# The first layer of a two-layer decoder trunk: operators on VectorE, state products on column parts by turns, a finer and new order of steps

## The chip, the cores and the metric

One Trainium2 chip (trn2), of which the kernel uses one core. The metric is device time in microseconds (us) of one execution, the median of several. The kernel is one launch; weights and activations are float32 in device memory.

## The reference

The reference computes two layers on one sequence of 256 tokens of width 1024, with 256 memory tokens. Each layer is a mixing part and a gated feed-forward block with a causal convolution over three tokens; every part starts from an RMS norm.

- Layer 0 mixes by a diagonal state-space layer (S5) on 768 of the 1024 columns: 48 groups of 16 channels with 64 complex states each. `y_t = Re(C s_t) + d u_t`, `s_t = A s_(t-1) + B u_t`, then `y = gelu(y)` and `y * sigmoid(y @ w_glu)`.
- Layer 1 mixes by causal attention of 12 heads on keys and values of its own.
- In both layers the other 256 columns are four heads of attention to the memory tokens: `softmax(q k^T / 8) v`, with keys and values `rms_norm(mem) @ w_mem_kv`.
- The two parts are joined, multiplied by `w_out` and added to the residual `x`; then `x + (silu(g) * v) @ w_down` with `g, v` from the convolution of `rms_norm(x) @ w_up`.

## The kernel before, in words

Activations lie with the 1024 features on partitions (8 tiles of 128) and the 256 tokens on the free axis. A float32 weight tile is split into an upper half `whi` (ScalarE, L115) and the rest `wlo` (VectorE, L119, or L121 where a gain is multiplied in), and a product is three matmuls (L249 to L251). Weights whose key stands in `NATIVE` are not split: one matmul in native float32, which the trace shows as two records. `Stream` (L82 to L136) loads weight tiles in a fixed list `order` (L199 to L205), two ahead, and splits them four ahead.

Layer 0 (`layer0`, from L590) works in these steps; the letters in brackets are those of the list `ORDER` (L43 to L48).

- Coefficients (L679 to L745) on VectorE: the decay, phase and input factors of the 24 pairs of groups. Powers of the phase factor (`E0`, `E1`; L778 to L801) for 8 and for 16 pairs, in four rounds, the fourth the largest; before, E0 is on VectorE, E1 on GpSimd.
- For each of three sets b of 8 pairs: the input operators (`Xr`, `Xi`; L747 to L758), two products and two sums each; the same transposed on TensorE (`T`, `t`; L766 to L776); the output operators (`V`; L803 to L819), two products and one sum of 128x1024, all nine on GpSimd before.
- The local operator (`l`, L821 to L843): per pair two products of 64 columns and one with the diagonal, into a 32-column part of the array; `L` copies it into place.
- The projection `x @ w_in` (`P`, native; L863 to L873), the mixer input (`u`), its placement (`U`, 16 copies per set, L880 to L889), the states (`S`): matmuls L896 and L897, rotation, two scans, rotation back and sums into `Hs` (L891 to L928).
- The outputs (`Y`): products of `U` with the local operator (L941) and of `Hs` with the output operator (L944) into two column halves, one half after the other; copies, transposes, gelu (`G`).
- Memory keys and values of layer 0 (`K`, native) and of layer 1 (`K1`, split; `m` splits the memory tokens for it), the queries (`q`) and the four memory heads (`A`: `attend`, L493 to L500): scores, softmax (L432 to L452), transposes, and the product with the values (L470, L471), each head alone in its column half.

Inside `tc.manual_schedule` TensorE, VectorE and GpSimd issue their instructions in just this list's order; ScalarE and everything outside it are placed by the scheduler, by priority. The gate with `w_glu`, the output projection and the residual follow outside the list. Layer 1 (L1085 on) has its own list `ORDER1`, placed by priority throughout.

Of the kernel before, what the change touches and what calls it, by code (L numbers as in the profile page):

```python
# [19 lines left out]
T = 256  # L20
# [11 lines left out]
NATIVE = (("mkv", 0), ("win", 0))  # L32
# [23 lines left out]
T_ACT = ((0, 0), (0, 1), (1, 0), (1, 1), (2, 0), (2, 1))  # L56
U_ACT = ((1, 1, 1, 0), (0, 1, 1, 1), (1, 0, 1, 1))
# [4 lines left out]
I I r1 X I I I r2 X I I I r3 Q0 qm Q1 h0 Q2 Q1 h2 K h0 K K X X h3 h2 K h1 R0 h1 h2 K K v v Q0 R1 R0 h3 R1 h0 h4 h5  # L62
h1 h3 v R2 v h7 e0 h10 Q2 h4 h6 h5 h8 h9 h7 h4 v v v h11 R2 v h2 h10 h6 h9 h13 h4 h5 h1 h14 h8 h6 h10 h0 h8 h12 h6
h7 h12 h3 O h11 h7 h13 h9 h14 h11 e1 h8 h12 h15 h15 h9 h13 h10 h12 h14 h13 h15 h5 h11 O O h15 h14 O O z1 O O O z0 z2
z3
"""
ST_DVE = [('k', 1)]
# [72 lines left out]
def _body(ctx, tc, a):  # L140
# [58 lines left out]
    order = [(("win", 0, ks, h), blocks(a["w_in"][0], ks, 512 * h, 512), (len(ks), 512)) for ks, h in W0]  # L199
    order += [(("mkv", l, c), mkv_ap(l, c), (2, 512)) for l in range(2) for c in range(4)]  # L200
    order += [(("glu", ks, b), blocks(a["w_glu"], ks, 256 * b, 256), (3, 256)) for ks, b in GLU]
    order += wout(0) + ffn_order(0) + win(1)
    order += [(("wk", ks, b), blocks(a["w_kv"], ks, 256 * b, 256), (4, 256)) for ks, b in WK]
    order += [(("wv", ks, c), blocks(a["w_kv"], ks, SELF + 384 * c, 384), (2, 384)) for c in range(2) for ks in PAIRS]
    order += wout(1) + ffn_order(1)  # L205
# [161 lines left out]
    def mem_kv(l, bk, mh, ml, ks, new, vm):  # L367
        pk, pv = bk(), bk()
        for k in range(KT):
            if k % 2 == 0:  # L370
                w = W.get(("mkv", l, k // 2))
            o = 512 * (k % 2)
            g = [m if m is None else m[k // 2][:, k % 2] for m in (mh, ml)]
            pairs = [(i, j) for i, j in ((0, 0), (0, 1), (1, 0)) if w[i] is not None and g[j] is not None]
            for m in range(2):
                for i, j in pairs:
                    PE.matmul(pk[:, 256 * m:256 * m + 256], w[i][:, o + 128 * m:o + 128 * m + 128], g[j],  # L377
                              start=k + m + i + j == 0, stop=k == KT - 1, skip_group_check=True)
            for t in range(2):
                for i, j in pairs:  # L380
                    PE.matmul(pv[:, 256 * t:256 * t + 256], g[j][:, 128 * t:128 * t + 128],  # L381
                              w[i][:, o + 256:o + 512], start=k + t + i + j == 0, stop=k == KT - 1,
                              skip_group_check=True)
            yield
# [47 lines left out]
    def softmax(sl, p, causal):  # L432
# [10 lines left out]
        for t in range(2):  # L443
            K = 128 * (t + 1) if causal else 256
            S.activation(P[:, t, :K], p[:, 256 * t:256 * t + K], AF.Exp, bias=nm[:, t:t + 1], scale=HD ** -0.5,
                         accum_out=su[:, t:t + 1])
        r = sm.tile([128, 2], F32, name="r")
# [4 lines left out]
        return P  # L452
# [20 lines left out]
    def head(h, sl, bs, bt, bo, q, k, v, causal, outp, hi, lo):  # L473
# [9 lines left out]
        if i not in outp:  # L483
            outp[i] = [bo("psO"), 0]
# [8 lines left out]
    def attend(heads):  # L493

        n = len(heads)
        for s in range(n + 3):
            for d in range(4):
                if 0 <= s - d < n:
                    next(heads[s - d])
# [771 lines left out]
```

## Time and profile before

| | us |
|---|---|
| median of 3 runs | 694.61 (694.43 to 701.04) |
| the profiled execution | 695.04 |
| its span, first to last instruction | 693.3 |
| TensorE busy | 654.1 (94%) |
| VectorE busy | 565.4 (82%) |
| ScalarE busy | 413.2 (60%) |
| GpSimd busy | 132.9 (19%) |

The profiled execution is one run of the same program with the hardware profiler on. Matmul records overlap (they are pipelined), so their cost is read from start to start, not from their durations. The granted clock of TensorE is given as a share of 2.4 GHz: 0.50 is 1.2 GHz, and a stretch with a value between has some of both.

### The profile page before, as it was taken

Reading aid. Unit: us, or ns where it says so; the run is one execution under the profiler, and the core shown is the slowest. Engines: PE = TensorE matmul, PEld = TensorE weight load, DVE = VectorE, ACT = ScalarE, POOL = GpSimd, SP = SyncE. Lnnn points to the kernel's source line nnn. Section 1 sums busy time; section 2 is a strip of 40 time slices with the busy share of each in tenths; the row PEclk is TensorE's granted clock in tenths of the full one; section 3 lists DMA queues with packets and bytes.
Section 4 is the critical chain, followed back from the end, with each engine's and each line's share of the span. In section 5 each row is a group of like instructions: output and inputs, shape, how many; then the busy total and the mean of one; then the engine's idle time right before and its main releaser. Section 6 shows DMA issues by size and latency. Waiting matters only on the chain.

```text
span 693.3 us, 12668 instructions
## 1 busy us (share of the span) xinstructions
PE 654.1 (94%) x4904; PEld 616.5 (89%) x4904; DVE 565.4 (82%) x1012; ACT 413.2 (60%) x747; POOL 132.9 (19%) x134
## 2 busy tenths in 40 slices
PE   6369899999999999999999998989999999999995
PEld 5358888998899999999999997868999999999984
DVE  7996999796879998888888798974749999888872
ACT  6368625576556665555557579864636666555631
POOL 5795623402300000000001255500300000000000
PEclk9775879999999999999999999899999999999998
DMA  8610133274455555555555544323625555565401
GB/s 315 245 62 1 61 99 99 93 217 148 152 181 184 183 183 181 186 185 182 182 186 156 168 128 140 107 89 122 213 92 182 181 186 183 183 188 187 172 1 61
DMA packets 43259, 105.13 MB, mean 152 GB/s; under 512 B 3776, under 2 KB 14144, under 8 KB 43200
## 3 DMA queue, kind: packets, MB, share of 16 engines
q1 hardware_dynamic: 42624, 103.74, 45.9%
q8 instruction: 38, 0.62, 0.4%
q10 hardware_dynamic: 576, 0.59, 0.2%
q14 instruction: 21, 0.17, 0.1%
HBM read 103.28 MB, written 1.05 MB: 150 GB/s over the span
## 4 chain that ended last, share of the span: by engine, by line
PE 82%; DVE 12%; DMA 2%; issue 2%; ACT 1%; POOL 0%; SPq 0%; DVEq 0%; ACTq 0%
PE psU L250 12%; PE psU L251 12%; PE psU L249 12%; PE acc L557 9%; PE acc L249 7%; PE acc L250 7%; PE acc L251 7%; PE ps L377 2%; DVE wlo L119 2%; PE ps L381 2%; PE ps L838 1%; DMA s5c<-s5b 1%; PE psO L470 1%; DVE X L638 1%; PE psT L458 1%
## 5 line engine op out<-in xcount | busy, mean ns | idle before, releaser
L115 ACT ACTIVATE whi<-wraw 128x1024 fp32r<-128x1024 f32 (+1 forms) x176 | 182.9, 1042 | 142.4 <-PE psU L250 84.9
L119 DVE TENSOR_TENSOR wlo<-wraw,whi 128x1024 fp32r<-128x1024 f32 (+1 forms) x176 | 217.9, 1240 | 26.7 <-PE acc L251 13.1
L250 PE MATMUL psU<-xlo,whi 128*128 128x256 f32 x704 | 198.6, 282 | 1.4 <-DVE xlo L331 1.4
L251 PE MATMUL psU<-xhi,wlo 128*128 128x256 f32 x704 | 197.8, 282 | 0.0
L249 PE MATMUL psU<-xhi,whi 128*128 128x256 f32 x704 | 197.6, 282 | 0.0
L250 PEld LDWEIGHTS psU<-xlo,whi 128*128 128x128 f32 x704 | 132.9, 189 | 2.5 <-DVE xlo L331 1.8
L249 PEld LDWEIGHTS psU<-xhi,whi 128*128 128x128 f32 x704 | 132.7, 189 | 0.7
L251 PEld LDWEIGHTS psU<-xhi,wlo 128*128 128x128 f32 x704 | 132.6, 189 | 0.0
L528 DVE SCALAR_TENSOR_TENSOR y<-u,held,y 128x254 f32<-128x254 f32 (+1 forms) x176 | 77.8, 477 | 1.5 <-ACT y L526 1.5
L521 DVE TENSOR_TENSOR u<-psU,rb 128x512 f32<-128x512 f32 x44 | 30.3, 688 | 32.4 <-PE psU L251 31.3
L526 ACT ACTIVATE y<-u,held 128x256 f32<-128x256 f32 x88 | 47.6, 589 | 13.0 <-DVE u L521 12.9
L269 POOL TENSOR_TENSOR sq<-sq 128x512 f32<-128x512 f32 x5 | 8.0, 1598 | 226.9 <-DVE held L364 179.1
L251 PE MATMUL acc<-ah,wlo 128*128 128x256 f32 x176 | 49.7, 283 | 0.0
L250 PE MATMUL acc<-al,whi 128*128 128x256 f32 x176 | 49.7, 283 | 0.0
L249 PE MATMUL acc<-ah,whi 128*128 128x256 f32 x176 | 49.6, 282 | 0.0
L869 PE MATMUL acc<-xg,wraw 128*128 128x256 f32 x128 | 34.1, 429 | 5.5 <-ACT xg L859 5.5
L869 PEld LDWEIGHTS acc<-xg,wraw 128*128 128x128 f32 x128 | 27.7, 221 | 10.0 <-ACT xg L859 5.5
L288 POOL TENSOR_TENSOR y<-mf,held 128x1 f32<-128x1 f32 x2 | 1.1, 550 | 180.5 <-DVE mf L1215 180.5
L249 PEld LDWEIGHTS acc<-ah,whi 128*128 128x128 f32 x176 | 33.6, 191 | 0.0
L251 PEld LDWEIGHTS acc<-ah,wlo 128*128 128x128 f32 x176 | 33.5, 191 | 0.0
L250 PEld LDWEIGHTS acc<-al,whi 128*128 128x128 f32 x176 | 33.5, 191 | 0.0
L250 PE MATMUL acc<-xlo,whi 128*128 128x256 f32 x112 | 31.7, 284 | 0.0
(271 smaller groups left out, 1475.1 us busy)
## 6 DMA issues: line engine op xcount, KB each, us to landing
wraw<-w_up SPq DMA_DIRECT2D x88, 512.0 KB, 3.4
wraw<-w_down SPq DMA_DIRECT2D x44, 512.0 KB, 3.4
wraw<-w_out SPq DMA_DIRECT2D x16, 512.0 KB, 3.6
wraw<-w_in SPq DMA_DIRECT2D x15, 512.0 KB, 3.5
wraw<-w_mem_kv SPq DMA_DIRECT2D x8, 512.0 KB, 4.2
wraw<-w_kv SPq DMA_DIRECT2D x6, 512.0 KB, 3.7
wraw<-w_kv SPq DMA_DIRECT2D x8, 384.0 KB, 3.4
wraw<-w_glu SPq DMA_DIRECT2D x6, 384.0 KB, 3.5
```

The lines of the kernel that those rows point to most:

```text
L115: self.nc.scalar.activation(hi[:, c], t[:, c], AF.Copy, scale=1.0 if g_ is None else g_)
L119: self.nc.vector.tensor_sub(lo[:, c], t[:, c], hi[:, c].bitcast(F32))
L249: PE.matmul(out, whi, ahi, start=first, stop=False, skip_group_check=True)
L250: PE.matmul(out, whi, alo, start=False, stop=False, skip_group_check=True)
L251: PE.matmul(out, wlo, ahi, start=False, stop=last, skip_group_check=True)
L377: PE.matmul(pk[:, 256 * m:256 * m + 256], w[i][:, o + 128 * m:o + 128 * m + 128], g[j], start=k + m + i + j == 0, stop=k == KT - 1, skip_g ...
L381: PE.matmul(pv[:, 256 * t:256 * t + 256], g[j][:, 128 * t:128 * t + 128], w[i][:, o + 256:o + 512], start=k + t + i + j == 0, stop=k == KT ...
L521: V.tensor_mul(u, v2(p), rb2(rb))
L526: S.activation(y[:, j], u[:, j], AF.Identity, bias=cp(3), scale=cp(2))
L528: V.scalar_tensor_tensor(y[:, j, d:], u[:, j, :T - d], cp(2 - d), y[:, j, d:], op0=ALU.mult, op1=ALU.add)
L557: PE.matmul(dacc[2 * t + h], a_, w_[:, 512 * i:512 * i + 512], start=False, stop=last and a_ is al, skip_group_check=True)
L869: PE.matmul(acc[2 * h + b][:, 256 * (m % 2):256 * (m % 2) + 256], w[:, 512 * i + 128 * m:512 * i + 128 * m + 128], xg[k // 2][:, k % 2], s ...
```

## The change

- Engines: the output operators' products go to VectorE, but for the sum of set 2; the first three rounds of E1 stay on GpSimd and its fourth goes to VectorE, the fourth of E0 goes to GpSimd; of the input operators the real half of set 2 is now GpSimd's instead of the imaginary half of set 0. All of the sums into `Hs` are on VectorE. Copies move between ScalarE and VectorE: eight of the twelve place copies that VectorE had go to ScalarE, one operator half (two copies), one `yc` copy and two `yT` copies go to VectorE.
- States, outputs and local operator are issued by turns on column parts of the array: states as two products of 64 columns each, outputs with the two halves alternating, the local operator over four 32-column parts. The diagonal comes ready from the host, as a 128-row table, instead of being multiplied out on VectorE.
- The second layer's memory projection becomes native: no split of its weights, no split of the memory tokens.
- Order: a new list, with finer steps (projection by halves, powers, output operators, local operator, outputs, softmax in two pieces). The gate, output projection and residual are in the list too. What stands behind the mark `|` is placed by priority. Weight loads are listed by the steps; their order comes out the same.
- Heads: two heads of a pair issue their value products together, alternating between the column halves, in both layers. Layer 1's list is as before but for the doubled softmax step, the pair steps `p` and the steps `x` for its first split.

```diff
-NATIVE = (("mkv", 0), ("win", 0))
+NATIVE = (("mkv", 0), ("mkv", 1), ("win", 0))
 ORDER = """
-P rm0 E0 P rx1 E1 P rx2 E0 P rx3 Xi0 Xr0 E0 V1 u0 t0 V0 V0 Xi1 u1 P B0 T0 D0 V0 Xr1 V1 U1 U0 P U0 l0 U0 T1 E1 U0 E1
-E1 Xi2 Xr2 E0 U1 S0 V1 P t2 S0 T2 S0 L0 U1 L0 P B1 L0 V2 t1 S0 D1 u2 U1 V2 U2 U2 U2 m S1 U2 S2 K S1 K K D2 K rm1 V2
-S1 B2 q l1 S1 L1 L1 rm2 L0 S2 Y0 S2 m S2 K K K K rm3 Y0 K L1 L1 G0 m K1 Y1 G0 Y2 Y1 K1 K1 m Y2 K1 G1 G2 K1 K1 G1 K1
-A G2 A A A A K1 A K1 A
+P E0 P P E1 P P P rm0 E0 Xr0 rx1 P P P rx2 E0 rx3 E0 E1 P Xi0 u0 D0 P U0 T0 U0 P U0 t0 P E1 D2 Xr1 P U0 V0 B0 Xi1 S0
+u1 V0 V0 l0 T1 Xi2 U1 S0 P U1 S0 l0 V2 V1 P V1 L0 V2 t1 K Xr2 B1 S0 L0 T2 U1 K u2 V1 rm1 U2 K U2 U1 L0 L0 Y0 B2 K U2
+t2 U2 E1 S1 V2 l1 D1 l1 l1 l1 L1 rm2 L1 S1 rm3 S2 Y0 S1 S1 K L1 K S2 K S2 Y0 L1 S2 K K1 Y1 K G0 G0 | q Y2 Y2 h1 Y1 h2
+Y1 h1 h3 h3 K1 K1 h0 Y2 h2 G1 h1 G2 h0 K1 K1 h0 K1 G1 h2 G2 h3 h1 h2 h0 K1 h3 K1 g g g g g p1 g0 g0 g g1 p0 g1 p1 K1
+g2 p0 o o o o g2 o o o o z3 z2 z1 z0
 """
-X_POOL = ((0, 1),)
-E_POOL = (1,)
-M_POOL = (1, 2, 3)
-H_DVE = (1,)
-V_DVE = ()
-Y_ACT = (0, 1, 2)
-EVAC_ACT = (0, 1, 2)
-T_ACT = ((0, 0), (0, 1), (1, 0), (1, 1), (2, 0), (2, 1))
-U_ACT = ((1, 1, 1, 0), (0, 1, 1, 1), (1, 0, 1, 1))
+V_POOL = ((2, 2),)
+X_POOL = ((2, 0),)
+E_POOL = ((0, 3), (1, 0), (1, 1), (1, 2))
+H_DVE = (0, 1, 2)
+Y_ACT = (1,)
+EVAC_ACT = (0, 2)
+T_ACT = ((0, 0), (0, 1), (1, 1), (2, 0), (2, 1))
+U_ACT = ((1, 1, 1, 0), (1, 1, 1, 1), (1, 1, 1, 1))
...
-    def pv(out, off, v, PT, causal):
-        c = 128 if causal else 0
-        PE.matmul(out[off:off + 64, :256], v[0], PT[:, 0], start=True, stop=False, skip_group_check=True)
-        PE.matmul(out[off:off + 64, c:256], v[1], PT[:, 1, c:], start=False, stop=True, skip_group_check=True)
+    def pv(out, pair, causal):
+        for t in range(2):
+            c = 128 if t and causal else 0
+            for h in range(2):
+                v, PT = pair[h]
+                PE.matmul(out[64 * h:64 * h + 64, c:256], v[t], PT[:, t, c:], start=t == 0, stop=t == 1,
+                          skip_group_check=True)
...
             for f in range(nf):
+                o = [p[32 * s:32 * s + 32, 128 * f:128 * f + 128] for s in range(4)]
+                for g in range(2):
+                    for s in range(4):
+                        PE.matmul(o[s].rearrange("p (i c) -> p i c", c=32)[:, :, 16 * g:16 * g + 16],
+                                  Bz[i][:, 4 * f + s, g], Vd[i][:, 4 * f + s, g, 0:4], start=g == 0, stop=False,
+                                  tile_position=(0, 32 * s), skip_group_check=True)
                 for s in range(4):
...
+                    PE.matmul(o[s][:, :32], ident[:, 32 * s:32 * s + 32], dsk[:, PC[i][0] // 4 + f], start=False,
+                              stop=True, tile_position=(0, 32 * s), skip_group_check=True)
+                yield
...
             for j in range(8):
-                PE.matmul(pr[:, 64 * j:64 * j + 64], RT[b][0][:, j], U[b][:, j], start=True, stop=True)
-                PE.matmul(pi[:, 64 * j:64 * j + 64], RT[b][1][:, j], U[b][:, j], start=True, stop=True)
+                for ri, p in enumerate((pr, pi)):
+                    for c in HALF:
+                        PE.matmul(p[c, 64 * j:64 * j + 64], RT[b][ri][:, j, c], U[b][:, j], start=True, stop=True,
+                                  tile_position=(0, c.start), skip_group_check=True)
...
-            for f in range(2):
-                for s in range(4):
-                    j = 4 * f + s
...
+            for s in range(4):
+                o = [py[64 * f:64 * f + 64].rearrange("p (i s c) -> p s i c", s=4, c=32)[:, s] for f in range(2)]
+                for f in range(2):
+                    PE.matmul(o[f], U[b][:, 4 * f + s], Tm[pc][:, off + 4 * f + s], start=s == 0, stop=False,
+                              tile_position=(0, 64 * f), skip_group_check=True)
+                for g in range(2):
+                    for f in range(2):
+                        PE.matmul(o[f][:, :, 16 * g:16 * g + 16], Hs[b][:, 4 * f + s, g],
+                                  Vd[pc][:, off + 4 * f + s, g, 1:5], start=False, stop=True,
+                                  tile_position=(0, 64 * f), skip_group_check=True)
...
+        by_hand, by_priority = ORDER.split("|")
+        with tc.manual_schedule(engines=MANUAL):
+            steps(by_hand)
+        steps(by_priority)
```

## Rows read from the trace of the kernel before

**Rows 1.** The page, section 4: the chain that ended last, by engine.

```profile
PE 82%; DVE 12%; DMA 2%; issue 2%; ACT 1%; POOL 0%; SPq 0%; DVEq 0%; ACTq 0%
```

**Rows 2.** Busy time by stretch: PE, PEld, DVE, ACT, POOL, granted clock, DMA.

```profile
60.00:80.00 20.00, 20.00 (x105) 18.38 (x104) 15.06 (x19) 11.82 (x28) 13.64 (x11) 0.73 0.16 46
80.00:100.00 20.00, 18.16 (x89) 16.41 (x88) 19.10 (x22) 9.47 (x22) 11.13 (x10) 0.74 0.22 74
```

**Rows 3.** Timeline of VectorE: start, us, engine, line, operation, count.

```profile
23.72 0.42 DVE L728 TENSOR_TENSOR s5c<-ct 128x72 f32<-128x72 f32 x2
...
28.98 3.00 DVE L638 TENSOR_TENSOR xt<-s5c 128x512 f32<-128x512 f32 x2
32.01 4.62 DVE L638 TENSOR_TENSOR X<-xt 64x512 f32<-64x512 f32 x2
...
46.25 1.31 DVE L638 TENSOR_TENSOR xt<-s5c 128x512 f32<-128x512 f32 x2
47.59 1.40 DVE L638 TENSOR_TENSOR X<-xt 64x512 f32<-64x512 f32 x2
...
58.34 0.19 DVE L638 TENSOR_TENSOR ee<-E 128x16 f32<-128x16 f32 x1
...
59.89 1.05 DVE L638 TENSOR_TENSOR E<-et 128x168 f32<-128x168 f32 x4
...
108.31 0.68 DVE L903 TENSOR_TENSOR rot<-ps,E 128x512 f32<-128x512 f32 x1
...
116.54 2.33 DVE L925 TENSOR_TENSOR H<-rot 64x504 f32<-64x504 f32 x2
```

**Rows 4.** Timeline of TensorE, the first feed-forward matmuls.

```profile
183.07 0.28 PE L249 MATMUL psU<-xhi,whi 128*128 128x256 f32 x1
183.19 0.28 PE L250 MATMUL psU<-xlo,whi 128*128 128x256 f32 x1
```

**Rows 5.** Timeline of GpSimd, two output-operator products.

```profile
29.10 4.66 POOL L635 TENSOR_TENSOR Vd<-s5c 128x1024 f32<-128x1024 f32 x2
```

**Rows 6.** The page, section 5: lower halves of weights on VectorE.

```profile
L119 DVE TENSOR_TENSOR wlo<-wraw,whi 128x1024 fp32r<-128x1024 f32 (+1 forms) x176 | 217.9, 1240 | 26.7 <-PE acc L251 13.1
```

**Rows 7.** Timeline of TensorE, states of set 1 and local operator of 16 pairs.

```profile
79.08 0.39 PE L897 MATMUL ps<-U,RT 128*128 128x64 f32 x2
79.30 0.39 PE L896 MATMUL ps<-U,RT 128*128 128x64 f32 x2
...
100.58 0.41 PE L838 MATMUL ps<-Vd,Bz 128*32 128x64 f32 x4
...
101.10 0.41 PE L838 MATMUL ps<-Vd,Bz 128*32 128x64 f32 x4
```

**Rows 8.** Timeline of TensorE, outputs of set 0 at the change of column half.

```profile
109.47 0.39 PE L944 MATMUL psY<-Vd,H 128*64 128x64 f32 x4
109.70 0.39 PE L941 MATMUL psY<-Tm,U 128*64 128x128 f32 x2
...
109.92 0.32 PE L941 MATMUL psY<-Tm,U 128*64 128x128 f32 x1
...
110.09 0.50 PE L944 MATMUL psY<-Vd,H 128*64 128x64 f32 x5
110.42 0.38 PE L941 MATMUL psY<-Tm,U 128*64 128x128 f32 x2
```

**Rows 9.** Timeline of TensorE, value products of two memory heads of layer 1.

```profile
448.83 0.66 PE L470 MATMUL psO<-PT,held 128*64 128x256 f32 x4
449.31 0.61 PE L471 MATMUL psO<-PT,held 128*64 128x256 f32 x4
```

**Rows 10.** Timeline of TensorE, native memory projection, two k steps.

```profile
115.43 1.03 PE L377 MATMUL ps<-memT,wraw 128*128 128x256 f32 x4
...
117.16 1.03 PE L377 MATMUL ps<-memT,wraw 128*128 128x256 f32 x4
```

**Rows 11.** Timeline of TensorE's weight loads for rows 9.

```profile
448.82 0.20 PEld L470 LDWEIGHTS psO<-PT,held 128*64 128x64 f32 x4 [0.25 <-issue]
```

More of the change, by code (lines that the diff above doesn't have):

```diff
@@ L198, in _body, with by_steps @@
     W0 = [((0,), 0), ((1,), 0)] + [(ks, h) for h in range(2) for ks in PAIRS][1:]
[L199 to L205, printed above, removed]
+    def by_steps(steps, **lists):
+        its = {n: iter(l) for n, l in lists.items()}
+        return [w for s_ in steps.split() if s_ in its for w in next(its[s_], ())]
+    one = lambda l: [[w] for w in l]
+    w0 = [(("win", 0, ks, h), blocks(a["w_in"][0], ks, 512 * h, 512), (len(ks), 512)) for ks, h in W0]
+    mkv = lambda l: [[(("mkv", l, k // 2), mkv_ap(l, k // 2), (2, 512))] if k % 2 == 0 else [] for k in range(KT)]
+    glu = [(("glu", ks, b), blocks(a["w_glu"], ks, 256 * b, 256), (3, 256)) for ks, b in GLU]
+    order = by_steps(ORDER, P=[w0[:2], []] + [p for w in w0[2:] for p in ([w], [])], K=mkv(0), K1=mkv(1), g=one(glu),
+                     o=one(wout(0)))
+    order += ffn_order(0)
+    order += by_steps(
+        ORDER1, I=one(win(1)),
+        K=one([(("wk", ks, b), blocks(a["w_kv"], ks, 256 * b, 256), (4, 256)) for ks, b in WK]),
+        v=one([(("wv", ks, c), blocks(a["w_kv"], ks, SELF + 384 * c, 384), (2, 384)) for c in range(2) for ks in PAIRS]),
+        O=one(wout(1)))
+    order += ffn_order(1)
     W = Stream(nc, order, rawp, hlp, lambda key: [gains[:, 2 + key[1], 2 * key[2] + i:2 * key[2] + i + 1]
@@ L370, in mem_kv @@
             if k % 2 == 0:
[L371 to L374, printed above, removed]
+                w, _ = W.get(("mkv", l, k // 2))
+            o, mk = 512 * (k % 2), mem[k // 2][:, k % 2]
             for m in range(2):
[L376 to L378 removed]
+                PE.matmul(pk[:, 256 * m:256 * m + 256], w[:, o + 128 * m:o + 128 * m + 128], mk, start=k + m == 0,
+                          stop=k == KT - 1, skip_group_check=True)
             for t in range(2):
[L380 to L383, printed above, removed]
+                PE.matmul(pv[:, 256 * t:256 * t + 256], mk[:, 128 * t:128 * t + 128], w[:, o + 256:o + 512],
+                          start=k + t == 0, stop=k == KT - 1, skip_group_check=True)
             yield
@@ L1000, in layer0 @@
             gens[f"Y{b}"] = outputs(b)
[L1001 removed]
+            gens[f"V{b}"] = output_operator(b, sc[1])
             gens[f"U{b}"] = by_place(b)
@@ L1050, in layer0, with steps @@
                 calls[f"{n}{b}"] = lambda f=f, b=b: f(b)
+        gens["g"], gens["o"] = gate(), output0()
+        for b in range(3):
+            gens[f"g{b}"] = gated(b)
+        for b in range(4):
+            calls[f"z{b}"] = lambda b=b: residual0(b)
         for i in range(2):
-            calls[f"l{i}"] = lambda i=i: local_operator(i)
+            gens[f"l{i}"] = local_operator(i)
             gens[f"L{i}"] = put_local_operator(i)
-        with tc.manual_schedule(engines=MANUAL):
-            for s in ORDER.split():
+        def steps(text):
+            for s in text.split():
                 if s in gens:
```

187 lines of the change are left out of this document (79 added, 108 removed).

## The prediction

> **What bounds the kernel now.** I read the chain of waits first. It puts 82% of the span on TensorE and 12% on VectorE [rows 1]; the two feed-forward blocks are matmuls end to end, the diff leaves them alone, and I count nothing there. So I cut the first 200 us into stretches: in 60 to 100 us TensorE looks busy nearly all the time, but its granted clock is only 0.73 and 0.74, that is, a mix of the levels 1.2 and 2.4 GHz, while VectorE is busy for 34 of the 40 us and GpSimd for 25 [rows 2]. The engine timelines then give the two halves of the first layer, and I use two marks to part them. Mark A is the end of the last state product of set 2 on VectorE, 116.54 + 2.33 = 118.9 us [rows 3]. Mark B is the first feed-forward matmul, 183.07 us [rows 4]. Up to A the order is set by VectorE, which starts behind the coefficients at 24.1 us [rows 3]; from A to B TensorE has no gap in its timeline: 64.2 us of matmuls.
>
> **VectorE up to A, step by step.** First its prices, taken where GpSimd is quiet. Half an input operator (Xr or Xi) is two products and two sums: 1.31 + 1.40 = 2.7 us; the same beside GpSimd's long products took 3.00 + 4.62 = 7.6 us [rows 3]. So a long GpSimd instruction costs VectorE more than the work it takes over: two output-operator products on GpSimd took 4.66 us [rows 5], and a 128x1024 product on VectorE takes 1.24 us [rows 6]. The fourth round of powers for 8 pairs took from 58.34 to 60.94, 2.6 us; for 16 pairs I take 4.5, bounds 2.6 (all fixed cost) and 5.2 (all size). One set of states took 108.31 to 116.54 = 8.2 us up to its last sums, and those are now four sums on VectorE, each as long as the 128x512 product at 108.31, 0.68 us: 2.7, together 10.9 us a set [rows 3].
>
> The list in the new order, from 24.1 us to the new A:
> - second and third round of E0: 3.6 (ten instructions of about 0.18 us each, the small ones in [rows 3]);
> - five halves of the input operators, as many as before but other ones: 5 x 2.7 = 13.5;
> - eight output-operator products and sums moved from GpSimd: 8 x 1.2 = 9.6;
> - fourth round of E1: 4.5;
> - three sets of states: 3 x 10.9 = 32.7;
> - three mixer inputs, two operator copies and one output copy of 128x512 at about 0.65: 3.9; one place copy of four instructions instead of twelve: 1.5;
> - two roots with GpSimd's power between them: 4.0 (an estimate; the power alone holds VectorE for about 1 us).
>
> That is 73.3 us. GpSimd keeps one fourth round, one half input operator and one output sum, about 11 us by the prices in [rows 5] and by size, and by the two prices of an input operator VectorE loses about half of that: 6. New A: 24.1 + 73.3 + 6 = 103.4 us, 15.5 earlier. In exchange go the lower halves of the second layer's memory weights (eight instructions), the memory split and the diagonal products; they stand in front of A today and are not in the list. Bounds: 97 with no loss to GpSimd; 137 if the operators run at the disturbed prices (five halves at 7.6, eight products at 2.4: 34 us more).
>
> The order of the weight loads stays as it is, and in 60 to 100 us the DMA engines are busy for 0.16 and 0.22 of the time [rows 2], so a stretch that gets shorter by a sixth finds its weights; the larger diagonal table is one more load of some 100 KB ahead of tables that are needed late.
>
> What ScalarE takes on (eight place copies, fewer evacuations) is hidden as long as it stays under VectorE's list; without that cover the place copies of set 0 would delay the first states by some 2 us.
>
> **TensorE.** Its products get shorter where column parts run side by side.
> - States: two records take 0.22 us, so 32 records cost 3.6 us a set at 2.4 GHz [rows 7]. After the change there are 64 records of half the width.
> - Local operator: a pair, six records, takes 0.52 us at 2.4 GHz [rows 7]; 24 pairs cost 12.3.
> - Outputs: six records take from 109.47 to 109.92, 0.45 us [rows 8], so 48 cost 3.6 us a set.
>
> What does running by turns give? The trace shows it once per set, where the outputs pass from one column half to the other: the first U product of the second half starts at 109.92, just when the last four records of the first half are due, and ten records are through by 110.42 [rows 8]. The last four ran alone, 0.22 us, so the six before them took 0.28 instead of 0.45. The other witness is longer: two heads whose value products the scheduler happened to put next to each other took at most 1.09 us for eight records [rows 9], where eight records in a row take 1.73 (the native projection, rows 115.43 to 117.16 [rows 10]). So the factor lies between 0.5 and 0.63 where it was seen; the other end is 1, no gain. I take 0.55 for two parts and 0.3 for four (estimates; the four-part bound is 0.25 to 1): states and outputs 3 x 1.6 each, local operator 8.6 less. That is 18.2 us of matmuls at 2.4 GHz, 16.6 of them ahead of A (all but the outputs of set 2). Only what stands behind A is counted directly; the rest keeps TensorE off VectorE's path.
>
> Against it, the second layer's memory projection becomes native: a k step costs 1.73 us [rows 10] instead of twelve products at 0.118 (start to start [rows 4]) = 1.42, so 8 x 0.31 = +2.5.
>
> **From A to B.** If nothing else moves ahead of A, what is left is: outputs of set 2 2.0, transposes 0.9, seven k steps 12.1, scores 1.9, head transposes 1.8, two head pairs 2.0 (four single heads cost 4 today), gate 108 x 0.118 = 12.7, output projection 192 x 0.118 = 22.6: 56.0 us. B would be 159.4. The other bound: TensorE has some 64 us of matmuls ahead of A in 98 us, so the seven k steps and the heads could fill its gaps; with all 17.8 us of them gone and 3 us of waiting for the last gate input, 41.2, B would be 144.6. VectorE's own list behind A (gelu, weight splits, heads, gates) comes to about 37 us, so it does not bind first. Since TensorE pays part of its gaps at 1.2 GHz, I take the nearer end: 4 us move ahead. B = 103.4 + 52 = 155.4, 27.7 us earlier; bounds 24 and 38.
>
> **Second layer.** Pairing head products looks like sixteen halved heads, but it mostly exists: both memory pairs and three of the six causal pairs already run as in [rows 9]. Three pairs remain. A causal head is two records of 256 columns, 0.216 us each by [rows 10], and two of half that: 0.65 us, with its changeover some 0.8; each pair hides one: 2.4 us. A pair must now wait for its slower head, and softmax is issued in two pieces, so the stage may shift by itself: bounds -6 and +4.
>
> **Sum.** 693.3 - 27.7 - 2.4 = 663.2 us of span; the profiled execution has 1.74 us around its span, so 664.9. It stands 0.4 above the median of the runs shown; I predict 664.5.
>
> **Rivals.**
> 1. *Column parts don't overlap for short products.* For: the witnesses are one boundary of six records and products of 256 columns. Against: four loads of 64 columns are all done 0.20 us after the first begins [rows 11], so even the loads run beside each other. Then the 18.2 us come back; TensorE has 64 + 16.6 = 81 us ahead of A, at a mean clock of 0.8 101 from 5 us on, and with stalls A is about 112; the tail is 60: B = 172, time 683. 8%. A worse form: load and product of a short record add up. The local operator's records, 0.086 us each [rows 7], show such a price; 64 of them are 5.5 us a set instead of 3.6, 48 are 4.1 instead of 3.6, together 7 us more: 690. 2%. The Trainium skill (TensorE: Matmul & The Clock Gate, section Part 3, on packing small matmuls) states the rule behind this form: a weight load overlaps a running product only where the row groups differ, and column parts share theirs. The four loads take 0.20 us while the first products of rows 9 run from 448.83 on, so the trace of before goes against the rule.
> 2. *Half clock.* TensorE gets more gaps while it waits for VectorE, and its clock is no higher than 0.73 there today [rows 2]. At a mean of 0.6 from 25 us on, its 50 us of remaining work ahead of A take 83 and with some 5 us of stalls end at 113; tail 56: B = 169, time 678. For: a shorter list of matmuls leaves longer gaps. Against: it is then also less often the one that is waited for. 12%.
> 3. *Slower: VectorE's queue.* All moved products stand in one ordered queue in front of the scans. If they run at the disturbed price (7.6 instead of 2.7 us for a half operator, 2.4 instead of 1.2 for a product), A goes to 137, the later bound, and B, with the 56 us behind it, to 193: time 705. It decides from A = 183.1 - 56 = 127 us on. For: VectorE is busy for 19 of 20 us already [rows 2]. Against: GpSimd keeps few long instructions. 3%.
> 4. *All fillers fit.* B at the early bound, 38 us gained, and 5 in the second layer: 650. 13%.
>
> **Chances.** The forecast keeps 62%. Range 648 to 684: it holds the forecast, rivals 2 and 4 and the milder end of rival 1. About 1% is what a measurement of this kernel can tell from no change. Faster by more: 91%; within: 5%; slower: 4%.
>
> **What would show it.** Right: the states of a set take about 2 us at 2.4 GHz and the local operator of 16 pairs 2 to 3; long input operators on VectorE at 2.7 us; A near 103 and B near 155; feed-forward blocks unchanged. Wrong: A later than 112 (then look whether VectorE is full or waits for TensorE), half-clock stretches from 40 to 100 us as long as today's, or column parts whose records start as far apart as one part's.

## The result and the profile after

The changed kernel takes 675.08 us (median of 4 runs, 673.70 to 677.59). The kernel before, run beside it, takes 694.83 (694.43 to 701.04). The ratio is 0.970, interval 0.964 to 0.976, so the kernel is 19.8 us faster. The prediction said 664.5 with 648 to 684: the direction and the range hold, the size is 10.6 us too good. The profiled execution has a span of 672.7 us and takes 674.49.

The chain that ended last, by engine, in the profile page of the changed kernel (before: [rows 1]):

```profile
PE 74%; DVE 18%; ACT 3%; issue 2%; POOL 1%; DMA 1%; DVEq 0%; ACTq 0%; POOLq 0%
```

VectorE's share went up from 12 to 18%, though it now does less: more of the path hangs on it. The same two marks as in the prediction show where. The first product of the feed-forward block (mark B, before: [rows 4]), and the last state product of set 2 on VectorE (mark A), in the timelines of the changed kernel:

```profile
167.40 0.28 PE L260 MATMUL psU<-xhi,whi 128*128 128x256 f32 x1
```

```profile
108.50 0.68 DVE L925 TENSOR_TENSOR H<-rot 64x504 f32<-64x504 f32 x1
```

A moved from 118.9 to 109.2 (predicted 103.4), B from 183.07 to 167.40 (predicted 155.4). Now both stretches, from 24.1 us to A and from A to B. The columns are the stretch, its length, then the busy time of TensorE, its weight loads, VectorE, ScalarE and GpSimd, then the granted clock, the DMA share and GB/s. First the kernel before:

```profile
24.10:118.90 94.80, 76.99 (x477) 67.06 (x478) 86.89 (x126) 52.01 (x126) 56.57 (x60) 0.77 0.22 69
118.90:183.07 64.17, 64.17 (x557) 61.22 (x556) 49.55 (x73) 41.54 (x74) 15.99 (x16) 1.00 0.49 160
```

and the changed kernel:

```profile
24.10:109.20 85.10, 69.30 (x690) 59.84 (x689) 75.41 (x121) 52.55 (x131) 33.92 (x49) 0.86 0.21 64
109.20:167.40 58.20, 52.96 (x425) 49.51 (x425) 48.50 (x73) 38.84 (x69) 12.52 (x10) 0.97 0.56 189
```

Read the third busy column first. Up to A VectorE does 75.4 us of work instead of 86.9, and stands still for 9.7 us (7.9 before). Behind A TensorE has 53.0 us of work instead of 64.2, near the 52 predicted, but it is no longer busy throughout: 5.2 us of gaps. VectorE's work there is 48.5 us. It was 49.6 before, hidden behind 64 us of matmuls. The two windows that answer to [rows 2]:

```profile
60.00:80.00 20.00, 9.70 (x78) 8.21 (x78) 19.83 (x26) 8.36 (x22) 4.15 (x3) 0.81 0.23 78
80.00:100.00 20.00, 19.88 (x301) 17.57 (x298) 17.44 (x33) 15.28 (x37) 1.36 (x4) 0.93 0.09 23
```

From 60 to 80 us TensorE now has less than half to do, and VectorE is full.

What each engine waited for from 20 us on, in the waits of the changed kernel (total, times, longest). VectorE up to 130 us:

```profile
DVE uT L874 <- ACT rb L1015: 3.2, 1, 3.2
DVE RT L780 <- PE ps L775: 2.1, 1, 2.1
DVE t L301 <- POOL y L299: 1.7, 2, 0.8
DVE rot L902 <- PE ps L895: 1.5, 1, 1.5
```

and TensorE up to 170 us:

```profile
PE psY L943 <- DVE H L925: 9.7, 3, 7.9
PE psS L431 <- DVE qs L412: 3.0, 1, 3.0
PE ps L834 <- DVE Vd L642: 2.7, 1, 2.7
PE acc L260 <- ACT yh L977: 1.2, 1, 1.2
```

TensorE's long wait (7.9 us before the outputs of set 0) stands ahead of A, where it costs VectorE at most the 1.5 us before the states of set 1. Its wait of 3.0 us for the queries of the heads stands behind A, on the path.

Behind B the span is 4.9 us shorter: from the first feed-forward product to the second layer's first input product 189.2 us instead of 191.9 (1.4 of it are two waits of TensorE for VectorE at the start of the block that are gone; the other 1.3 stays unexplained), the second layer's mixing 118.9 instead of 121.8, the rest 197.1 instead of 196.5.

### The profile page after: what moved, and what is told of

Its sections match the earlier page's. It is cut to its first block, busy times and chain, and to the rows that moved or that the text cites. A ratio compares the mean times of both kernels' runs of the same rounds, so it can differ in the third digit from the quotient of the medians.

```text
span 672.7 us, 12639 instructions
## 1 busy us (share of the span) xinstructions
PE 628.6 (93%) x4968; PEld 594.6 (88%) x4968; DVE 545.1 (81%) x1009; ACT 407.4 (61%) x746; POOL 109.6 (16%) x119
## 4 chain that ended last, share of the span: by engine, by line
PE 74%; DVE 18%; ACT 3%; issue 2%; POOL 1%; DMA 1%; DVEq 0%; ACTq 0%; POOLq 0%
PE psU L262 12%; PE psU L260 12%; PE psU L261 12%; PE acc L562 9%; PE acc L261 7%; PE acc L260 7%; PE acc L262 7%; DVE wlo L119 2%; ACT P L451 1%; DVE X L642 1%; DVE xt L642 1%; PE psO L481 1%; DVE Vd L642 1%; DVE cf L649 1%; ACT sw L1138 1%
## 5 line engine op out<-in xcount | busy, mean ns | idle before, releaser
L119 DVE TENSOR_TENSOR wlo<-wraw,whi 128x1024 fp32r<-128x1024 f32 (+1 forms) x176 | 215.7, 1229 | 10.7 <-ACT whi L115 7.7
L115 ACT ACTIVATE whi<-wraw 128x1024 fp32r<-128x1024 f32 (+1 forms) x176 | 180.5, 1033 | 65.8 <-PE psU L261 34.0
L262 PE MATMUL acc<-ah,wlo 128*128 128x256 f32 x176 | 49.6, 282 | 0.0
L537 ACT ACTIVATE th<-y 128x256 f32<-128x256 f32 x44 | 18.2, 415 | 30.6 <-DVE y L533 30.6
```

The costliest lines, as they stand in the source:

```text
L115: self.nc.scalar.activation(hi[:, c], t[:, c], AF.Copy, scale=1.0 if g_ is None else g_)
L119: self.nc.vector.tensor_sub(lo[:, c], t[:, c], hi[:, c].bitcast(F32))
L262: PE.matmul(out, wlo, ahi, start=False, stop=last, skip_group_check=True)
L537: S.activation(th, g, AF.Tanh, scale=0.5)
```

## The experiments

All are edits of the changed kernel. For each: the median, A and B (us). B compares first layers better than the time does, because the medians also carry what the second layer's clock does (at the end). A and B come from one profile of each run, so small differences need care. In the run with the second layer as before the first layer's code is that of the changed kernel, and still A is 1.9 earlier, at the same B. Two things that no edit was aimed at stand in the table beside the marks: the granted clock from A to B, and VectorE's wait for the scale (ScalarE's copy of it, L1015 in the changed kernel) ahead of the first mixer input. That wait is 3.2 us in some runs and 0.8 or 0.9 in the others, and why ScalarE's copy waits for GpSimd in the first and not in the second was not looked into.

| run | time | A | B | clock from A to B | wait for the scale |
|---|---|---|---|---|---|
| before | 694.8 | 118.9 | 183.1 | 1.00 | 0 |
| changed | 675.1 | 109.2 | 167.4 | 0.97 | 3.2 |
| column parts in line | 677.3 | 110.9 | 170.6 | 0.97 | 3.2 |
| output operators on GpSimd | 675.2 | 112.7 | 168.6 | 1.00 | 0.8 |
| long operators all on VectorE | 673.1 | 107.5 | 164.8 | 1.00 | 0.8 |
| projection steps ahead | 674.9 | 104.9 | 165.7 | 0.94 | 0.8 |
| second projection split | 676.9 | 114.6 | 172.6 | 0.94 | 3.2 |
| old order and engines | 690.7 | 112.2 | 178.8 | 0.95 | 0 |
| the same, two steps moved | 683.5 | 110.1 | 178.1 | 0.90 | 0 |
| second layer as before | 676.8 | 107.2 | 167.4 | 0.91 | 3.2 |
| both edits | 684.9 | 114.0 | 174.2 | 0.94 | 0.8 |
| steps before the transposes | 677.6 | 108.6 | 169.1 | 0.94 | 0.9 |
| heads ahead | 678.8 | 120.2 | 170.5 | 0.94 | 0.8 |
| copies on ScalarE | 668.6 | 105.5 | 162.0 | 1.00 | 0.8 |

**Column parts in line again.** The states, and likewise the outputs (half after half) and the local operator (pair after pair):

```diff
                 for ri, p in enumerate((pr, pi)):
-                    for c in HALF:
-                        PE.matmul(p[c, 64 * j:64 * j + 64], RT[b][ri][:, j, c], U[b][:, j], start=True, stop=True,
-                                  tile_position=(0, c.start), skip_group_check=True)
+                    PE.matmul(p[:, 64 * j:64 * j + 64], RT[b][ri][:, j], U[b][:, j], start=True, stop=True)
```

> The changed kernel with the column parts in line again: states as products of 128 columns, outputs half after half, the local operator pair after pair. By the durations in its trace this gives TensorE about 20 us more at 2.4 GHz (states 3 x 1.7, local operator 9.8, outputs 3 x 1.9). Theory 1 (VectorE's list sets mark A, so the parts only keep TensorE off its path): only what stands in front of a wait of VectorE counts, about 2.8 us before the operator copies at 52 us, 3.6 before the states of set 1 and 1.9 for the last outputs: about 683 us, 8 more. Rival (TensorE sets the time up to A, so what the parts save is saved one for one): about 18 us more, 693.

Measured: 677.31 us (ratio to before 0.970, 0.964 to 0.975), 2.2 us more by the medians where the first theory expected 8; B 3.2 later, at the same clock and the same wait for the scale. The first theory holds in kind, with much less than it expected. TensorE's timeline of this run, states of set 1 and two pairs of the local operator:

```profile
84.68 3.68 PE L893 MATMUL ps<-U,RT 128*128 128x64 f32 x32
...
88.57 0.30 PE L834 MATMUL ps<-Vd,Bz 128*32 128x64 f32 x4
...
88.72 0.30 PE L834 MATMUL ps<-Vd,Bz 128*32 128x64 f32 x4
```

and of the changed kernel, the same states and two groups of four pairs:

```profile
84.46 2.08 PE L895 MATMUL ps<-U,RT 128*64 128x64 f32 x64
86.48 0.43 PE L834 MATMUL ps<-Vd,Bz 128*32 128x64 f32 x16
...
86.79 0.41 PE L834 MATMUL ps<-Vd,Bz 128*32 128x64 f32 x16
...
87.07 0.41 PE L834 MATMUL ps<-Vd,Bz 128*32 128x64 f32 x16
```

The turns do what they say: 64 records of 64 columns in 2.08 us against 32 of 128 columns in 3.68, and four pairs of the local operator every 0.29 us against one every 0.15. With the outputs (3.4 us a set here from the first start to the last, 1.8 in turns in the run with projection steps ahead, both at 2.4 GHz) that is 3 x 1.6 + 3 x 1.6 + 24 x 0.08, some 11 us of TensorE, and it is worth 3.2 at B. But look at the local operator in line: 0.15 us a pair, where it took 0.52 before [rows 7]. The turns are not what made it cheap; the last section comes back to that.

**Output operators on GpSimd.**

```diff
-V_POOL = ((2, 2),)
+V_POOL = tuple((b, r) for b in range(3) for r in range(3))
```

> The changed kernel with all nine output-operator products and sums on GpSimd, as before the change. Theory (long GpSimd instructions beside VectorE's cost it more than the work they take over): VectorE is spared 8 x 1.2 = 9.6 us and loses about as much as GpSimd is busy, 8 x 2.33 = 19: about 685 us, 10 more. Rival (who executes the products is indifferent, the gain of the change came from the work that was dropped): 675 us, within 2.

Measured: 675.19 us (0.968, 0.962 to 0.974), B 1.2 later: the rival holds for the time. The theory's price is there, though. VectorE is spared 9.6 us of products, but its busy time up to A falls only from 75.4 to 72.8; and its list now stands for 11.5 us behind TensorE, which waits for GpSimd's products (waits of this run):

```profile
PE ps L834 <- POOL Vd L639: 7.2, 1, 7.2
```

```profile
DVE RT L780 <- PE ps L775: 11.5, 1, 11.5
```

A is 3.5 later. What evens it out: VectorE has less to do, the wait for the scale is 0.8 us instead of 3.2 (the copy on ScalarE does not wait for GpSimd's powers here), and behind A the clock is 1.00 instead of 0.97. Neither of the last two is what the edit was about, so the 1.2 at B may be too small a price; the 2.4 us of the wait, if they reached B in full, would make it 3.6.

**Long operators all on VectorE.**

```diff
-V_POOL = ((2, 2),)
-X_POOL = ((2, 0),)
-E_POOL = ((0, 3), (1, 0), (1, 1), (1, 2))
+V_POOL = ()
+X_POOL = ()
+E_POOL = ((1, 0), (1, 1), (1, 2))
```

> The changed kernel with everything long that GpSimd kept put on VectorE: the fourth round of the 8 pairs, half an input operator, one output sum. VectorE gets 2.8 + 2.7 + 0.7 = 6.2 us of work. Theory (GpSimd's long instructions and the wait for its powers are what put A 5.8 us later than predicted): the 3.2 us wait before the first mixer input goes, the two disturbed halves of an input operator lose 3.8 and the sums beside it some 2: A about 3 earlier, 672 us. Rival (work adds up, contention is small): A 6 later, 681 us.

Measured: 673.09 us (0.964, 0.959 to 0.969), A 1.7 and B 2.6 earlier. The theory holds in direction: VectorE does 6.2 us more of its own work, and its busy time up to A grows by 1.6 only, from 75.4 to 77.0:

```profile
24.10:107.54 83.44, 67.61 (x675) 57.55 (x676) 77.03 (x132) 52.00 (x130) 16.47 (x34) 0.89 0.20 65
```

The 2.4 us by which the wait for the scale shrinks are more than the 1.7 gained at A, and that wait shrinks in runs that leave the powers on GpSimd too; so the edit's own part of the gain is not shown. What is shown is the price. One half input operator on VectorE, two products and two sums, in the changed kernel beside the end of GpSimd's half operator and its sums of squares:

```profile
53.18 3.15 DVE L642 TENSOR_TENSOR xt<-s5c 128x512 f32<-128x512 f32 x2
56.37 3.32 DVE L642 TENSOR_TENSOR X<-xt 64x512 f32<-64x512 f32 x2
```

and the same instructions in this run, with GpSimd quiet:

```profile
53.53 1.28 DVE L642 TENSOR_TENSOR xt<-s5c 128x512 f32<-128x512 f32 x2
54.85 1.41 DVE L642 TENSOR_TENSOR X<-xt 64x512 f32<-64x512 f32 x2
```

6.5 us against 2.7. The Trainium skill (SBUF — State Buffer, section SBUF: two separate sides) says that an operation of VectorE with two inputs from SBUF and a GpSimd instruction that reads SBUF lock a shared port pair, and the second blocks until the first is through. The traces agree. In the run with the output operators on GpSimd, GpSimd works without a pause from 62.3 to 67.9 us; the products there that read one input from PSUM (L902 to L905) take their quiet 0.68 to 0.69 us, and the two sums behind them, with both inputs in SBUF, 1.40 and 1.75 instead of 0.68:

```profile
64.14 0.68 DVE L904 TENSOR_TENSOR rot<-ps,E 128x512 f32<-128x512 f32 x1
...
65.34 1.40 DVE L906 TENSOR_TENSOR rot<-rot 128x512 f32<-128x512 f32 x1
66.66 1.75 DVE L907 TENSOR_TENSOR rot<-rot 128x512 f32<-128x512 f32 x1
```

```profile
62.32 2.52 POOL L639 TENSOR_TENSOR xt<-s5c 128x512 f32<-128x512 f32 x2
64.91 2.95 POOL L639 TENSOR_TENSOR X<-xt 64x512 f32<-64x512 f32 x2
```

**Projection steps ahead.** Five of the first layer's eight projection steps (K) stand ahead of the outputs of set 0 (Y0), where TensorE was idle for 7.9 us:

```diff
-u1 V0 V0 l0 T1 Xi2 U1 S0 P U1 S0 l0 V2 V1 P V1 L0 V2 t1 K Xr2 B1 S0 L0 T2 U1 K u2 V1 rm1 U2 K U2 U1 L0 L0 Y0 B2 K U2
-t2 U2 E1 S1 V2 l1 D1 l1 l1 l1 L1 rm2 L1 S1 rm3 S2 Y0 S1 S1 K L1 K S2 K S2 Y0 L1 S2 K K1 Y1 K G0 G0 | q Y2 Y2 h1 Y1 h2
+u1 V0 V0 l0 T1 Xi2 U1 S0 P U1 S0 l0 V2 V1 P V1 L0 V2 t1 K Xr2 B1 S0 L0 T2 U1 K u2 V1 rm1 U2 K U2 U1 L0 L0 K K K K K Y0 B2 U2
+t2 U2 E1 S1 V2 l1 D1 l1 l1 l1 L1 rm2 L1 S1 rm3 S2 Y0 S1 S1 L1 S2 S2 Y0 L1 S2 K1 Y1 K G0 G0 | q Y2 Y2 h1 Y1 h2
```

> The changed kernel with five steps of the first layer's memory projection moved ahead of the outputs of set 0, where TensorE stands still for 7.9 us. Theory (VectorE sets both A and the stretch just behind it): the states of set 1 come some 3 us earlier, VectorE loses its wait of 1.5 us before them, little more comes out: 673 us, 2 less. Rival (the tail is matmuls, as predicted, and what is moved ahead comes off it): 668 us, 7 less.

Measured: 674.86 us (0.965, 0.960 to 0.971), A 4.3 and B 1.7 earlier. That is the little that the theory expected, but the rival was not put to the test, because no matmul left the tail. The matmuls that read the memory tokens, all of them steps of the two projections, in the stretches up to A and from A to B: first the changed kernel, then this run (stretch, length, TensorE's busy time on them and their number, clock, DMA):

```profile
24.10:109.20 85.10, 24.10 (x100) 0.86 0.21 64
109.20:167.40 58.20, 6.48 (x28) 0.97 0.56 189
```

```profile
24.10:104.90 80.80, 27.58 (x100) 0.89 0.25 78
104.90:165.66 60.76, 7.54 (x28) 0.94 0.49 168
```

In both, 100 records stand ahead of A and 28 behind it. In the changed kernel the five steps had run ahead of A already, one from 80.7 us on and four from 90.8; the edit moved them within the stretch up to A. Of the 4.3 us gained there 2.4 are the wait for the scale and 0.8 a wait for transposes (L780), both ahead of every moved step; 0.9 are the wait for the states of set 1. So what the steps themselves did to B is not shown. The tail grew from 58.2 to 60.8 us. In the changed kernel 14 of the 28 records stand right in front of the scores; here all stand behind the first scores, and TensorE waits longer for the queries, the next thing in VectorE's list (waits of this run from 100 to 166 us):

```profile
PE psS L431 <- DVE qs L412: 6.2, 1, 6.2
```

**Second projection split again.** The three split products per native one, the weight halves, and the memory split behind the states of set 1:

```diff
-NATIVE = (("mkv", 0), ("mkv", 1), ("win", 0))
+NATIVE = (("mkv", 0), ("win", 0))
```

> The changed kernel with the second layer's memory projection split into three products again (eight weight halves and one memory part on VectorE, three memory parts on GpSimd, four copies on ScalarE), its work put where the new order reaches it. Theory (VectorE's list is what the time follows, so the dropped split is one large part of the gain): VectorE gets 8 x 0.7 to 0.95 and 0.7, and loses some to GpSimd: 7 to 9 us more, about 683. Rival (the tail is TensorE's): the split products are 2.5 us shorter there than native ones: 672.5.

Measured: 676.89 us (0.971, 0.966 to 0.977), B 5.2 later where 7 to 9 were expected. The theory holds at B: VectorE's busy time from 24.1 us to B grows by 7.7 (123.9 to 131.6 us). The median gives only 1.8 of it: the second layer took 117.6 us in this profile instead of 118.9, and the rest of the difference lies within the scatter of the medians.

**Old order and engines.** The new code with the order string and the engine lists of before (steps that are finer now written twice), without the memory split. It leaves out the last of the gate's six weight blocks (18 products, 2.1 us at the distance of [rows 4]), so some 2.1 are to be added to its B and its time; that is an estimate, as the splitting of that block on ScalarE and VectorE is missing too.

> The code of the changed kernel (native projection, column parts, head pairs) run in the old order of the first layer and with the old choice of engines for the operators and copies. Theory (after the run with the output operators on GpSimd, which cost nothing: the new order is the larger part of the gain, the rest only takes work off engines that wait): 688 us, within 4. Rival (native projection and column parts carry the gain, the order little): 678 us or less.

Measured: 690.73 us (0.991, 0.988 to 0.994), B 178.8. The theory holds, with the 2.1 added by a little more than its 4 us. A second run put the last two steps of the second projection ahead of the heads; the gate's block is missing there too:

> The run of the new code in the old order again, with the last two steps of the second layer's projection ahead of the heads, so that all buffers keep their values until they are read. Both theories as there; nothing else moves: 690.7 us, within 2.

Measured: 683.46 us (0.977, 0.971 to 0.983), a miss in the time: 7.3 less. B is 0.7 earlier. Of the rest, 4.9 lie in the second layer, which took 117.8 us instead of 122.7. So order and engine lists are worth 10.7 to 11.4 us at B, and some 2.1 more with the gate's block: the largest part of the change. The two were not undone apart from each other: the lists alone put eight place copies and more back on VectorE.

**Second layer as before.** Single heads and the old order string of the second layer, the first layer as changed.

> The changed kernel with the second layer as before (single heads, old order). In the traces so far the stage from its first input product to the first product of its feed-forward block takes 121.7 before, 118.2 to 118.9 in three runs of after and its variants, and 122.0 and 122.2 in two others which show one more stretch at half clock some 90 us into the stage. Theory (pairs are worth under 1 us, the difference is that stretch): the stage takes 118.5 to 119.5 without that stretch or about 122 with it, time 675 within 2. Rival (three pairs give 2.4 us, as predicted): the stage takes 121.3 without the stretch, time 677.5.

Measured: 676.82 us (0.972, 0.967 to 0.976), the stage 121.8 us: the rival holds, my theory falls. B is the same to 0.01 us, while A is 1.9 earlier and the clock from A to B is 0.91 instead of 0.97: B does not hang on A alone. The stretch at half clock is there in both; 8 us windows, TensorE only (busy, granted clock, DMA share, GB/s), of this run

```profile
437.00:445.00 8.00, 8.00 (x39) 0.68 0.00 0
445.00:453.00 8.00, 8.00 (x57) 1.00 0.20 69
```

and of the changed kernel

```profile
412.60:420.60 8.00, 7.18 (x29) 0.57 0.39 131
444.60:452.60 8.00, 6.88 (x51) 1.00 0.49 174
```

One such stretch each, a mean granted clock of 0.97 over the stage in both, and the stage is 2.8 us shorter with pairs and the new order.

**Both edits, and two attempts to mend them.** The fourth and third run together:

> The two edits together: everything long on VectorE, and five projection steps ahead of the outputs of set 0. Apart they brought mark A from 109.2 to 106.9 and 104.2, and B from 167.4 to 164.8 and 165.7. Theory (both act through the same waits of VectorE, and VectorE is full behind A): A about 104, B about 164, time 671. Rival (they add up): A 102, B 163 or less, time 669 or less.

(The 106.9 and 104.2 named for A are the starts of the last product; the marks of the table, its ends, are 107.5 and 104.9.) Measured: 684.91 us (0.983, 0.978 to 0.988), slower than either by 10 or more: both theories fail. TensorE's queue is in order, and in it the steps stand behind the transposes (L775) of the half input operator that VectorE now makes late. In TensorE's timeline of this run, with the idle time before it in brackets:

```profile
70.14 1.94 PE L775 MATMUL ps<-held,X 128*128 128x128 f32 x8 [10.19 <-DVE X L642]
```

and in VectorE's, what that does to the states of set 1, which stand behind the five steps:

```profile
91.36 0.69 DVE L902 TENSOR_TENSOR rot<-ps,E 128x512 f32<-128x512 f32 x1 [7.73 <-PE ps L895]
```

So three of the steps went ahead of those transposes:

```diff
-u1 V0 V0 l0 T1 Xi2 U1 S0 P U1 S0 l0 V2 V1 P V1 L0 V2 t1 K Xr2 B1 S0 L0 T2 U1 K u2 V1 rm1 U2 K U2 U1 L0 L0 K K K K K Y0 B2 U2
+u1 V0 V0 l0 T1 Xi2 U1 S0 P U1 S0 l0 V2 V1 P V1 L0 V2 t1 K K K K Xr2 B1 S0 L0 T2 U1 K u2 V1 rm1 U2 K U2 U1 L0 L0 K K Y0 B2 U2
```

> Everything long on VectorE, and the projection steps moved ahead not only of the outputs of set 0 but also of the transposes that wait for VectorE's half input operator (in the run with both edits TensorE stood 10.2 us at these transposes with five steps queued behind them, and the states of set 1 came 7.7 us late). Theory (the order of TensorE's queue made that run slow, and VectorE's list limits the rest): no wait of VectorE for the states over 1 us, A near 106, B 163 to 165, time 671 to 673. Rival (matmul work moved ahead of A comes off the tail): B 160, time 668.

Measured: 677.63 us (0.969, 0.964 to 0.974), slower than both theories said. The wait for the states fell from 7.7 to 1.8 us, so the queue was the cause of the 7.7; but B stayed at 169.1, behind the 164.8 without the steps. A is 1.1 later than there, and behind A TensorE waits 6.2 us for the queries, as long as in the run with projection steps ahead; in the run with the long operators on VectorE, without the steps, it waits 2.6. A third run moved the queries, the keys and three steps of the second projection ahead of A as well:

> As the run before this, and also the queries of the first layer's heads, the last step of its memory projection and three steps of the second layer's projection ahead of A. Theory (the tail is VectorE's list of 48 us with TensorE waiting some 5 us for it; what leaves that list shortens it): VectorE does 2.1 us of the queries and 0.7 of the keys ahead of A, A about 108, TensorE's wait for the queries (2.6 us) goes, B about 161, time 669. Rival (VectorE is full ahead of A as well, so its work is only moved): A 109, B 164, time 672.

Measured: 678.84 us (0.971, 0.966 to 0.976), A 120.2, B 170.5: the rival's direction, and worse. This is the run in which matmuls did leave the tail:

```profile
24.10:120.20 96.10, 76.91 (x730) 65.21 (x729) 89.68 (x149) 59.39 (x141) 21.77 (x39) 0.89 0.31 101
120.20:170.48 50.28, 46.67 (x381) 43.46 (x381) 36.73 (x60) 32.41 (x59) 7.14 (x5) 0.94 0.39 127
```

VectorE's busy time ahead of A rose to 89.7 us and behind A fell to 36.7; its sum stayed (126.4 against 125.0 in the run before), and so, nearly, did the time.

**Copies on ScalarE.** Everything long on VectorE, and five copies of 128x512 from VectorE to ScalarE:

```diff
-Y_ACT = (1,)
-EVAC_ACT = (0, 2)
-T_ACT = ((0, 0), (0, 1), (1, 1), (2, 0), (2, 1))
+Y_ACT = (0, 1, 2)
+EVAC_ACT = (0, 1, 2)
+T_ACT = ((0, 0), (0, 1), (1, 0), (1, 1), (2, 0), (2, 1))
```

> Everything long on VectorE, and five copies moved from VectorE to ScalarE: two of the transposed input operator, two of the turned outputs, one output copy, 5 x 0.68 = 3.4 us. In the runs so far VectorE's busy time from 24.1 us to B is 82 to 89% of that stretch whatever was edited, while matmuls moved out of the tail did not shorten it. Theory (VectorE's list sets B): 3.4 us less of it at a share of 0.89 is 3.8: B 161, time 669.5, TensorE unchanged. Rival (B hangs on the waits between engines, and the way over ScalarE's queue adds some): B 165 or later, time 673 or more.

Measured: 668.62 us (median of 6; 0.9615, 0.957 to 0.966), B 162.0: the theory holds, and this is the fastest version, 6.5 us below the changed kernel by the medians; the two intervals against before still overlap a little, 0.964 to 0.966. Its two stretches, to be laid beside those of the changed kernel:

```profile
24.10:105.52 81.42, 67.85 (x685) 58.41 (x684) 76.26 (x137) 55.27 (x137) 16.46 (x34) 0.89 0.27 87
105.52:162.03 56.51, 53.88 (x433) 49.88 (x433) 48.81 (x72) 40.04 (x71) 12.68 (x10) 1.00 0.53 178
```

VectorE's idle time ahead of A is 5.2 us instead of 9.7, and the clock in the tail is 1.00. The run that differs from it by the copies alone is the one with the long operators on VectorE: against that one A is 2.0 and B 2.7 earlier at the same clock and the same wait for the scale, and of the 4.7 us between the two profiled executions 1.5 are the second layer's (117.3 us instead of 118.8). VectorE's busy time up to B did not fall by the copies' 3.4 (125.1 instead of 125.3), as other work of it moved in, one more half of a weight (1.8 us) among it; so that the list alone sets B is not shown, only that taking work off it moves B.

## Why the prediction came out as it did

By its own steps, in us of span:

- **VectorE's list up to A.** Predicted 73.3 of work and 6 lost to GpSimd, no idle time: 79.3. Measured 75.4 of work, losses included, and 9.7 of idle time. The prices were good where GpSimd is quiet: an output-operator product 1.17 to 1.23 (1.2 assumed), a half input operator 2.7, a set of states 11.0 (10.9), the fourth round for 16 pairs about 4.0 (4.5). The step that failed is that VectorE would never wait: A came 5.8 late. Each of its four waits (3.2, 2.1, 1.7, 1.5) hangs on another engine that the list did not model. Only the roots had been given some.
- **The tail.** Predicted 52 us of TensorE, measured 53.0. That they are so near is in part luck: the sum has seven steps of the projections there less 4 us, 8.1 us, and 28 records stand there, three and a half steps, 6 us by the same price; a stretch at half clock (granted clock 0.97) makes up for much of it. The step that failed is that TensorE would not wait in the tail, for "VectorE's own list behind A comes to about 37 us, so it does not bind first". It is 48.5, and one windows query on the kernel before would have given 49.6. With 53.0 and 48.5 us on two engines that wait for each other the stretch takes 58.2: 6.2 more than predicted. TensorE's list is still the longer one there; of its 5.2 us of gaps 3.0 are the wait for the queries. With five copies taken off VectorE and the long operators on it the gaps are 2.6 us and that wait is 0.7. How much of the 58.2 each list sets was not settled.
- **What carries the gain.** I had put it on VectorE's prices and the column parts. Undone one at a time, at B: order and engine lists 11 to 13, the split of the second projection 5.2, the column parts 3.2, output operators on VectorE 1.2, or up to 3.6 with the wait for the scale. They add to more than the 15.7 that were gained, since each covers for others. That a long GpSimd instruction costs VectorE more than it takes over is true of the instructions (6.5 against 2.7 us) and was worth little here, because VectorE also waited less.
- **Column parts.** Factor 0.55 for two parts: measured 0.57 for the states (2.08 of 3.68) and 0.53 for the outputs (1.8 of 3.4). Right, though the two witnesses gave 0.62 and 0.63, and its lower end of 0.5 was in no row. For the local operator the sum was near (3.7 predicted for 24 pairs, 1.7 measured), but its reason was not: see below.
- **The second layer.** 2.4 predicted, 2.8 measured, and 2.8 against the run with the old second layer, which is the cleaner comparison: the stage has two stretches at half clock in the kernel before (mean granted clock 0.96), one in the other two (0.97). Right.
- **The feed-forward blocks.** 0 predicted; 2.7 gained at the start of the first one, 1.4 of it explained by the two waits.

The misses add up: 5.8 at A, 6.2 in the tail, less 2.7, less 0.4, and 0.6 behind: 9.5 us, the distance between 663.2 and 672.7.

**The rivals.** No overlap of the parts: excluded, by the timelines above. Half clock: excluded for this stretch; the granted clock ahead of A is 0.86 instead of 0.77. Slower through VectorE's queue: its mechanism is at work (A late by contention and waits), far from its deciding point of 127. All fillers fit: they do not. In the run with the heads ahead all steps of both projections and the scores of the heads stand ahead of A, and A comes at 120.2 and B at 170.5, with VectorE busy for 89.7 of the 96.1 us up to A.

## What to carry to other kernels

Where two engines are both busy for over four fifths of a stretch, price the stretch for both, with the busy time of a window and not with a list from memory, and give the one that is waited for an idle share too: here 5 to 10 us in 85. Work taken off VectorE (five copies to ScalarE, 3.4 us) moved B by most of its size, 2.7, while the edits that filled TensorE's gaps moved it little or made it worse. Before a step is moved ahead of a mark, count in the trace on which side of the mark it stands now: the five projection steps stood ahead of A already, so moving them could take nothing off the stretch behind it. In a queue that is executed in order, a step moved ahead is only ahead if nothing in front of it waits: place it in front of that wait, not in front of the gap.

## What the runs showed of the hardware

**A change of row count between products.** The local operator of before puts a product over 32 rows (L841) between those over 128 rows, and takes 0.52 us a pair [rows 7]. In the run with the parts in line the order is the same, pair after pair, and the diagonal product runs over 128 rows with the same six records: 0.15 us a pair. The diagonal products of before and of that run:

```profile
100.92 0.24 PE L841 MATMUL ps<-dd,held 32*32 32x32 f32 x2
```

```profile
88.69 0.22 PE L837 MATMUL ps<-dsk,held 128*32 128x32 f32 x2
```

The granted clock was 1.00 in both stretches. No run changes the row count and nothing else, but in this stage the diagonal's operands are all that differs. So the larger diagonal table, which I had taken for one more load of 100 KB, saved 0.37 us a pair, 8.9 for 24 pairs, and the turns the remaining 0.08 of a pair. The Trainium skill (TensorEngine Tiling (Array Packing), section Key Properties) says that changing the tiling mode drains TensorE, while a change of tile within a mode does not; the runs agree with it, and I had not weighed that rule.

**Stretches at half clock come and go.** The second layer of the changed kernel shows one stretch at half clock some 55 us into its mixing stage, and in four of the profiled runs there is a second one about 90 us in, though its code is the same. Windows of the run with projection steps ahead, at the same places as those of the changed kernel above:

```profile
411.10:419.10 8.00, 6.41 (x30) 0.69 0.50 166
443.10:451.10 8.00, 7.00 (x28) 0.61 0.80 264
```

The stage takes 117.3 to 118.9 us with one such stretch and 122.0 to 122.7 with two. That is 3 to 5 us, as much as most edits here are worth, and it is why B and not the time told the first layer's versions apart. It differs between executions of one kernel too: the four of the run with projection steps ahead took 672.5 to 676.4 us, the shortest at a mean granted clock of 0.977 and the longest at 0.966. B is not free of it either, with 0.90 to 1.00 between A and B. What decides whether the second stretch comes was not tried.
